# A two-layer diffusion backbone: conditioning loads issued further ahead, with their products kept in written order, and a pause in attention

## The chip, the cores and the metric

The kernel runs on one core of one Trainium2 chip. The metric is the device time of one execution in microseconds, lower is better. TensorE (PE) does the matrix products, VectorE (DVE), ScalarE (ACT) and GpSimd (POOL) the rest. SyncE (SP) issues the loads of the network's weights, and ACT issues the loads of the conditioning weights from its own queue. Each engine works off its instructions in a fixed order, so an instruction that waits holds up everything behind it on its engine.

## The reference, cut to what matters

There are 256 latent tokens, 256 context tokens, a width of 2048 and two layers. Layer 0 mixes tokens by neighbourhood attention with 16 heads, layer 1 by a gated MLP (gMLP). A SwiGLU FFN of width 5632 follows each of them. Every sub-layer takes a shift, a scale and a gate from a conditioning vector:

```python
sh1, sc1, g1, sh2, sc2, g2 = split(silu(c) @ ada_w[i] + ada_b[i], 6)   # per layer i
a = h * (1 + sc1) + sh1
y = mixer(a)                      # attention in layer 0, gMLP in layer 1
h = layer_norm(ALPHA * h + g1 * y)
h = layer_norm(ALPHA * h + g2 * swiglu(h * (1 + sc2) + sh2))
```

The product with `ada_w` has one row on the left. It is some 12 million multiplications per layer and reads 100 MB of weights per layer, and this kernel gives most of it to DVE, not to PE.

## The kernel before, in words

**Precision and the weight pipeline.** Every large product is made of three TensorE products (`mm3`, lines 87 to 90): a float32 operand is split into a rounded part and a rest, and high by high, low by high and high by low are added. A weight tile of 128x1024 floats (512 KB) is loaded by SP (line 110) into one of four `raw` buffers, rounded by ACT (`split_into`, line 93, tiles `hw...`), and subtracted by DVE (line 94, tiles `lw...`). PE consumes the pair. There are three to five such pairs, so DVE and ACT can be up to about four tiles ahead of PE. In the names, `wq`, `wk`, `wv` are the projections, `wo` the attention's output, `wt` and `wf` the FFN's first matrix, `wd` its second, `wg` and `wgo` those of the gMLP.

**Stages.** First comes a prologue that makes layer 0's first shift and scale on PE and DVE and projects the first keys and values. Then come the attention heads with their projections, the output projection `wo` with residual and layer norm, FFN 0, the gMLP with its output `wgo`, FFN 1, and the store. An output projection (`project_out`) works on two halves of the output columns; between the first half and the second it needs the gate (`need(key)`, line 741), and it has its layer norm done per 128 tokens (`finish`).

**Conditioning tasks.** All other shifts, scales and gates are made of small tasks that stand in a list beside the main work. For a shift or scale, `dot_task` (line 142) multiplies a transposed 128x1024 tile of `ada_w` with the broadcast conditioning vector and adds up each row: one DVE instruction at line 152, tiles `ad`, with a short read of the accumulator behind it. A vector takes 32 of them, and 128x16 additions at the end. For a gate, `gate_task` (line 162) adds tile times column to an accumulator of 128x2048: one DVE instruction at line 176, tiles `ag`. After 32 of those, `sum_task` (line 188) adds the 128 partitions by one GpSimd instruction, `partition_all_reduce` (line 191). In a name such as `ad1061`, the digits are layer, vector (0 to 5 for SH1, SC1, G1, SH2, SC2, G2), tile and half.

`tick` (line 216) is called at each step of the main work. It adds to a credit that `pace` set so that the listed tasks are spread over so many steps, and runs a task for each half unit of credit. `fetch_ahead` (line 197) issues the loads of the first `FETCH` tasks in the list, so a load is written that many tasks ahead of its use. The buffers are `ADA` in number (line 76). A load waits on ACT's queue until its buffer is free. `need` runs all tasks up to the ones that it names at once.

**The order of the instructions.** The program is written in order, but a scheduler may move instructions of one engine past each other by priority and by when it believes their operands to be there. An instruction that goes through `keep_in_program_order` (`pin`, line 84) is left at its place. The loads of the conditioning tiles are pinned (line 77). The DVE instructions that use them aren't.

**Attention.** For each head, the key projection (from head 3 on) and the query projection are made in steps of one weight tile each. After each step `unit` (line 475) calls `tick`, and takes one stage of the attention from the list `pend`. A head has three stages: `scores` (scores on PE, bias and maximum on DVE, exponential on ACT, reciprocal on DVE, scaling on ACT, which leaves the probabilities `p`), `transpose` (eight 128x128 transposes on PE, tiles `pt`, line 552, then a split) and `values` (12 products of 256 columns, tiles `o`). At heads 3, 7 and 11 eight steps of value projection (`proj_v`) follow. After the last head the remaining stages are run without steps between them.

Of the kernel before, what the change touches and what calls it, by code (L numbers as in the profile page):

```python
# [15 lines left out]
ALU = mybir.AluOpType  # L16
# [21 lines left out]
SH1, SC1, G1, SH2, SC2, G2 = range(6)  # L38
HK0 = 3
RAW = 4  # L40
ADA = 4
FETCH = 3
BUSY = 0.3
DVE0 = 3
W0 = HK0 * P + 512
# [6 lines left out]
def hybrid_kernel(ctx: ExitStack, tc: tile.TileContext, i, out):  # L52
    nc = tc.nc
    V, S, T = nc.vector, nc.scalar, nc.tensor
# [29 lines left out]
    def pin(ins):  # L84
        return tc.keep_in_program_order(ins)
# [54 lines left out]
    loaded = {}  # L140

    def dot_task(layer, t, nt, half):
        key = (layer, t, nt, half)

        def fetch():
            src = i["ada_t"][dot_index(layer, t, nt)]
            loaded[key] = load(src[:, half * 1024 : (half + 1) * 1024], f"ad{layer}{t}{nt}{half}")

        def run():
            r = loaded.pop(key)  # L150
            o = (cols2 if half else cols)[:, layer, t, :]
            V.scalar_tensor_tensor(  # L152
                r, r, 1.0, c_bc[:, half * 1024 : (half + 1) * 1024], ALU.mult, ALU.mult,
                accum_out=o[:, nt : nt + 1],
            )
            if nt == KT - 1 and half:
                o = cols[:, layer, t, :]
                V.tensor_tensor(o, o, cols2[:, layer, t, :], ALU.add)
                V.tensor_tensor(o, o, badj[:, layer, t, :], ALU.add)
        return [(layer, t), 0.5, run, fetch]  # L160

    def gate_task(layer, t, kt, half):
        key = (layer, t, kt, half)
        sl = slice(half * 1024, (half + 1) * 1024)

        def fetch():
            if kt == 0 and half == 0:
                g = outer.tile([P, D], F32, tag="gate", name=f"gate{layer}{t}")
                gate[(layer, t)] = g
                nc.gpsimd.memset(g, 0.0)  # L170
                nc.gpsimd.dma_start(g[0:1, :], i["ada_b_row"][layer, t : t + 1, :])
            loaded[key] = load(i["ada_g"][gate_index(layer, t, kt)][:, sl], f"ag{layer}{t}{kt}{half}")

        def run():
            g = gate[(layer, t)][:, sl]
            V.scalar_tensor_tensor(g, loaded.pop(key), c_col[:, kt, 0:1], g, ALU.mult, ALU.add)  # L176
        return [(layer, t), 0.5, run, fetch]

    def act_split(src, name, at=None):
# [23 lines left out]
    def add_tasks(layer, *ts):  # L203
        for t in ts:
            if t in (G1, G2):
                tasks.extend(gate_task(layer, t, k, e) for k in range(KT) for e in range(2))
                tasks.append(sum_task(layer, t))
            else:
                tasks.extend(dot_task(layer, t, k, e) for k in range(KT) for e in range(2))
# [67 lines left out]
    with tc.tile_pool(name="attnX", bufs=1) as px, ExitStack() as late:  # L277
# [187 lines left out]
        def t_tile(name):  # L465
            return mp.tile([P, 512], F32, tag="t", name=name, bufs=2)

        add_tasks(0, G1, SH2, SC2)
        add_tasks(1, SH1)
        pace(126)  # L470
        pend = []
        with tc.tile_pool(name="attnB", bufs=1) as pb:
            qh, ql = {}, {}

            def unit(n=1.0):
                tick(n)
                if pend:
                    pend.pop(0)()

            def proj_q(h):  # L480
                ps = acc_tile(f"qps{h}")
# [42 lines left out]
            def attention(h):  # L524
# [42 lines left out]
                        mm3(ps[:, 0:NT], vh[:, kb, :], vl[:, kb, :], th[:, ks], tl[:, ks], kb == 0, kb == 3)  # L567
                    S.copy(oT[:, h, :], ps[:, 0:NT])

                return [scores, transpose, values]  # L570

            for h in range(NH):
                if h >= HK0:
                    proj_k(h)
                proj_q(h)
                if h in V_AT_Q:
                    while len(pend) > 3:
                        pend.pop(0)()
                    proj_v(V_AT_Q[h])
            while pend:  # L580
                pend.pop(0)()

    need((0, SH2), (0, SC2))
    main = ctx.enter_context(tc.tile_pool(name="main", bufs=1))
# [249 lines left out]
    )  # L834
    affine_tasks(h_t, i["ln_row"][0], "a0")
    add_tasks(0, G2)
    add_tasks(1, SC1, SH2, SC2)
    pace(245)
    m2 = []

# [199 lines left out]
```

## Time and profile before

| | us |
|---|---|
| median of 3 runs (2460.63 to 2463.62) | 2462.59 |
| profiled execution, its own time | 2464.19 |
| profiled execution, span of the core | 2462.4 |
| PE busy | 2388.5 (97%) |
| DVE busy | 1753.7 (71%) |
| ACT busy | 1120.5 (46%) |
| read from HBM | 606.46 MB |

In the trace each instruction has its engine, its line and its operands. In square brackets stands the idle time of the engine just before the instruction, and what ended it. Busy shares alone don't tell here what a step is worth: PE is busy nearly throughout, and what can be won is its idle time. For each idle stretch of PE one has to follow what came last, often through two engines.

### The profile page before, as it was taken

To read this page: it belongs to the slowest core of one execution; us is meant where nothing else is said; L and a number is where in the kernel's file an instruction comes from. 1 tells how busy PE (TensorE), PEld (TensorE's weight loads), DVE (VectorE), ACT (ScalarE), POOL (GpSimd) and SP (SyncE) were. 2 spreads that over 40 slices of the span, in tenths; PEclk is the share of its full clock that TensorE was granted. 3 is DMA by queue.
4 is the path that set the end of the run, shared out by engine and by line. 5 is a ranking of instruction groups with operands and counts; after the bars stand their busy time and mean duration, and the time that the engine had idled before them with its cause. 6 is when DMAs were issued, how large, how long until landed. Compare 5 with 4: busy or idle time off the path is not lost. (4 is left out here: it accounts for less than half of the span.)

```text
span 2462.4 us, 31266 instructions
## 1 busy us (share of the span) xinstructions
PE 2388.5 (97%) x11574; PEld 1979.4 (80%) x11574; DVE 1753.7 (71%) x2158; ACT 1120.5 (46%) x1534; POOL 110.3 (4%) x54
## 2 busy tenths in 40 slices
PE   7999999999999999999999999899999999999998
PEld 5788888888788888887888778777888888888886
DVE  4878877777887777666778778778755555566666
ACT  3344434335554444443455554445544444445453
POOL 0000200000010010000000010020100000020000
PEclk9999999999999999999999999999999999999999
DMA  9978787877578888887888767766567676766563
GB/s 358 346 248 266 254 288 260 273 253 246 188 241 284 293 280 299 284 290 275 280 290 283 247 208 263 241 210 196 199 229 229 226 227 225 230 198 190 178 211 131
DMA packets 167682, 610.63 MB, mean 248 GB/s; under 512 B 19076, under 2 KB 21572, under 8 KB 163172
## 3 DMA queue, kind: packets, MB, share of 16 engines
q1 hardware_dynamic: 120888, 440.64, 53.9%
q10 hardware_dynamic: 46512, 167.96, 19.9%
q8 instruction: 90, 1.47, 0.2%
q14 instruction: 64, 0.52, 0.1%
q0 software_dynamic: 128, 0.03, 0.0%
HBM read 606.46 MB, written 2.10 MB: 247 GB/s over the span
## 5 line engine op out<-in xcount | busy, mean ns | idle before, releaser
L93 ACT CAST hwf<-rwf 128x1024 fp32r<-128x1024 f32 x320 | 336.9, 1053 | 491.2 <-PE pu L90 206.0
L94 DVE TENSOR_TENSOR lwf<-rwf,hwf 128x1024 fp32r<-128x1024 f32 x320 | 404.3, 1277 | 173.8 <-ACT hwf L93 172.8
L152 DVE SCALAR_TENSOR_TENSOR ad<-ad,c_bc 128x1024 f32<-128x1024 f32 x192 | 234.0, 1222 | 168.9 <-DMA ad<-in_ada_t 168.3
L88 PE MATMUL pod<-hwd,ghd 128*128 128x512 f32 x684 | 267.3, 391 | 3.5 <-DVE sg L815 3.5
L90 PE MATMUL pod<-hwd,gld 128*128 128x512 f32 x684 | 266.5, 390 | 0.7 <-DVE gld L94 0.7
L89 PE MATMUL pod<-lwd,ghd 128*128 128x512 f32 x684 | 266.8, 390 | 0.0
L176 DVE SCALAR_TENSOR_TENSOR gate<-ag,c_col,gate 128x1024 f32<-128x1024 f32 x128 | 164.4, 1288 | 121.1 <-DMA ag<-in_ada_g 120.8
L94 DVE TENSOR_TENSOR lwd<-rwd,hwd 128x1024 fp32r<-128x1024 f32 x172 | 211.7, 1232 | 51.3 <-ACT hwd L93 51.0
L93 ACT CAST hwd<-rwd 128x1024 fp32r<-128x1024 f32 x172 | 180.3, 1049 | 33.3 <-PE pu L90 11.5
L88 PEld LDWEIGHTS pod<-hwd,ghd 128*128 128x128 f32 x684 | 128.7, 188 | 30.5 <-DVE sg L815 4.0
L90 PEld LDWEIGHTS pod<-hwd,gld 128*128 128x128 f32 x684 | 128.7, 188 | 28.1 <-DVE gld L94 1.2
L89 PEld LDWEIGHTS pod<-lwd,ghd 128*128 128x128 f32 x684 | 128.8, 188 | 26.6
L88 PE MATMUL pg<-hwf,f1h 128*128 128x512 f32 x320 | 126.4, 395 | 0.0
L88 PE MATMUL pg<-hwf,f0h 128*128 128x512 f32 x320 | 126.4, 395 | 0.0
L90 PE MATMUL pg<-hwf,f1l 128*128 128x512 f32 x320 | 124.7, 390 | 0.0
L90 PE MATMUL pg<-hwf,f0l 128*128 128x512 f32 x320 | 124.7, 390 | 0.0
L88 PE MATMUL pu<-hwf,f0h 128*128 128x512 f32 x320 | 124.5, 389 | 0.0
L89 PE MATMUL pu<-lwf,f0h 128*128 128x512 f32 x320 | 124.5, 389 | 0.0
L90 PE MATMUL pu<-hwf,f0l 128*128 128x512 f32 x320 | 124.5, 389 | 0.0
L88 PE MATMUL pu<-hwf,f1h 128*128 128x512 f32 x320 | 124.5, 389 | 0.0
L89 PE MATMUL pu<-lwf,f1h 128*128 128x512 f32 x320 | 124.5, 389 | 0.0
L90 PE MATMUL pu<-hwf,f1l 128*128 128x512 f32 x320 | 124.5, 389 | 0.0
(338 smaller groups left out, 5345.1 us busy)
## 6 DMA issues: line engine op xcount, KB each, us to landing
rwf<-in_w_in_t SPq DMA_DIRECT2D x320, 512.0 KB
ad<-in_ada_t ACTq DMA_DIRECT2D x192, 512.0 KB
rwd<-in_w_out SPq DMA_DIRECT2D x176, 512.0 KB
ag<-in_ada_g ACTq DMA_DIRECT2D x128, 512.0 KB
rwg<-in_w_gin SPq DMA_DIRECT2D x64, 512.0 KB
ap<-in_ada_p SPq DMA_DIRECT2D x19, 1024.0 KB
rwq<-in_w_q SPq DMA_DIRECT2D x32, 512.0 KB
rwo<-in_w_o SPq DMA_DIRECT2D x32, 512.0 KB
```

Of the source, the lines that this page charges most:

```text
L88: keep(T.matmul(ps, sh, mh, start=first, stop=False))
L89: keep(T.matmul(ps, sh, ml, start=False, stop=False))
L90: keep(T.matmul(ps, sl, mh, start=False, stop=last))
L93: S.copy(hi, src)
L94: V.tensor_tensor(lo, src, hi.bitcast(F32), ALU.subtract)
L152: V.scalar_tensor_tensor(r, r, 1.0, c_bc[:, half * 1024 : (half + 1) * 1024], ALU.mult, ALU.mult, accum_out=o[:, nt : nt + 1],)
L176: V.scalar_tensor_tensor(g, loaded.pop(key), c_col[:, kt, 0:1], g, ALU.mult, ALU.add)
```

## The change

Six things are edited.

1. `FETCH` goes from 3 to 5 and `ADA` from 4 to 6: a load is written five tasks ahead of its use, into one of six buffers. To make room in the memory on the chip, the descriptor area of GpSimd's DMAs is cut to 4096 bytes.
2. The DVE instruction of every dot and gate task is pinned.
3. The 32 dots of layer 1's SH1 leave the attention's list and stand in the list of FFN 0. The attention has 97 tasks where it had 129, FFN 0 has 161 where it had 129, over the same `pace`.
4. In the attention's list, gate G1 stands last; it stood first.
5. An empty stage stands between `scores` and `transpose`, so that a step's work is done between the two that wasn't.
6. Before a value projection, `pend` is cut to 8 stages, not to 3.

```diff
-ADA = 4
-FETCH = 3
+ADA = 6
+FETCH = 5
+SCRATCH = 4096
...
# dot_task.run()
-            V.scalar_tensor_tensor(
+            pin(V.scalar_tensor_tensor(
                 r, r, 1.0, c_bc[:, half * 1024 : (half + 1) * 1024], ALU.mult, ALU.mult,
                 accum_out=o[:, nt : nt + 1],
-            )
+            ))
...
# gate_task.run()
-            V.scalar_tensor_tensor(g, loaded.pop(key), c_col[:, kt, 0:1], g, ALU.mult, ALU.add)
+            pin(V.scalar_tensor_tensor(g, loaded.pop(key), c_col[:, kt, 0:1], g, ALU.mult, ALU.add))
...
# ahead of the attention
-        add_tasks(0, G1, SH2, SC2)
-        add_tasks(1, SH1)
+        add_tasks(0, SH2, SC2, G1)
         pace(126)
...
+            def advance():
+                stage = pend.pop(0)
+                if stage:
+                    stage()
+
             def unit(n=1.0):
                 tick(n)
                 if pend:
-                    pend.pop(0)()
+                    advance()
...
-                return [scores, transpose, values]
+                return [scores, None, transpose, values]
...
                 if h in V_AT_Q:
-                    while len(pend) > 3:
-                        pend.pop(0)()
+                    while len(pend) > 8:
+                        advance()
                     proj_v(V_AT_Q[h])
             while pend:
-                pend.pop(0)()
+                advance()
...
# ahead of the first FFN
     add_tasks(0, G2)
-    add_tasks(1, SC1, SH2, SC2)
+    add_tasks(1, SH1, SC1, SH2, SC2)
     pace(245)
...
-    nc = bacc.Bacc("TRN2", target_bir_lowering=False, num_devices=1)
+    nc = bacc.Bacc("TRN2", target_bir_lowering=False, num_devices=1, dynamic_dma_scratch_size=SCRATCH)
```

The diff alone doesn't tell what the scheduler made of it. Three places of the DVE order show it. Line numbers of the changed kernel are one higher from line 43 to 467 and five higher from line 480 on.

**DVE at head 12's softmax, before.** `ql12` is the split of the head's query, `s120` and `s121` its scores for two blocks of queries, `nm` their maxima, `sm` their sums:

```order
L493 SCALAR_TENSOR_TENSOR ql12_4588<-qps12_4523,qh12_4587 128x256
L152 SCALAR_TENSOR_TENSOR ad1061_4592,cols2_72<-ad1061_4592,c_bc_98 128x1024
L152 SCALAR_TENSOR_TENSOR ad1070_4626,cols_71<-ad1070_4626,c_bc_98 128x1024
L535 TENSOR_TENSOR s120_4633<-s120_4633,bias12_4631 128x256
L535 TENSOR_TENSOR s121_4645<-s121_4645,bias12_4631 128x256
L537 TENSOR_REDUCE nm120_4638<-s120_4633 128x1
L537 TENSOR_REDUCE nm121_4650<-s121_4645 128x1
L94 TENSOR_TENSOR lwq13_1024_4660<-rwq13_1024_4657,hwq13_1024_4659 128x1024
L152 SCALAR_TENSOR_TENSOR ad1071_4629,cols2_72<-ad1071_4629,c_bc_98 128x1024
L541 RECIPROCAL sm120_4640<-sm120_4640 128x1
```

The loads of `ad1061`, `ad1070` and `ad1071` stand next to each other on ACT, right behind the rounding of `qh12`, that is behind the instruction on which `ql12` waits:

```order
L93 CAST hwq13_0_4597<-rwq13_0_4595 128x1024
L492 ACTIVATE qh12_4587<-qps12_4523 128x256
L77 DMA ad1061_4592<-in_ada_t 128x1024
L77 DMA ad1070_4626<-in_ada_t 128x1024
L77 DMA ad1071_4629<-in_ada_t 128x1024
```

**DVE at the same place, after:**

```order
L498 SCALAR_TENSOR_TENSOR ql12_4513<-qps12_4451,qh12_4512 128x256
L177 SCALAR_TENSOR_TENSOR gate02_3798<-ag0280_4367,c_col_58,gate02_3798 128x1024
L177 SCALAR_TENSOR_TENSOR gate02_3798<-ag0281_4406,c_col_58,gate02_3798 128x1024
L177 SCALAR_TENSOR_TENSOR gate02_3798<-ag0290_4409,c_col_58,gate02_3798 128x1024
L540 TENSOR_TENSOR s120_4558<-s120_4558,bias12_4556 128x256
L542 TENSOR_REDUCE nm120_4563<-s120_4558 128x1
L540 TENSOR_TENSOR s121_4570<-s121_4570,bias12_4556 128x256
L542 TENSOR_REDUCE nm121_4575<-s121_4570 128x1
L95 TENSOR_TENSOR lwq13_1024_4585<-rwq13_1024_4582,hwq13_1024_4584 128x1024
L546 RECIPROCAL sm120_4565<-sm120_4565 128x1
```

The tasks are now gate tasks, three in a row ahead of `s120`. Their loads stand further up on ACT; the last of the three, and what lies between it and `qh12`:

```order
L78 DMA ag0290_4409<-in_ada_g 128x1024
L94 CAST hwq12_1024_4413<-rwq12_1024_4411 128x1024
L78 DMA ag0291_4442<-in_ada_g 128x1024
L78 DMA ag02100_4445<-in_ada_g 128x1024
L94 CAST hwk13_0_4454<-rwk13_0_4452 128x1024
L94 CAST kh12_4447<-kps12_4374 128x512
L94 CAST hwk13_1024_4484<-rwk13_1024_4482 128x1024
L94 CAST hwq13_0_4522<-rwq13_0_4520 128x1024
L497 ACTIVATE qh12_4512<-qps12_4451 128x256
```

Between the load of `ag0290` and the rounding of `qh12`, four weight tiles and the keys of head 12 are rounded; before, no weight tile stood between the load of `ad1061` and its use. Over the whole program, counted in weight tiles of 128x1024 that are rounded between a load and its use, the attention's tasks had a mean of 0.3 before and have 3.9 now, those of FFN 0 had 1.0 and have 7.4, those of the gMLP 1.6 and 10.9.

**DVE at the end of attention, before.** `s150` and `s151` are the scores of the last head, `lwo` a weight tile of the output projection:

```order
L152 SCALAR_TENSOR_TENSOR ad10150_5167,cols_71<-ad10150_5167,c_bc_98 128x1024
L94 TENSOR_TENSOR lwo0_2_0_5324<-rwo0_2_0_5321,hwo0_2_0_5323 128x1024
L493 SCALAR_TENSOR_TENSOR ql15_5218<-qps15_5135,qh15_5217 128x256
L535 TENSOR_TENSOR s150_5226<-s150_5226,bias15_5224 128x256
L535 TENSOR_TENSOR s151_5238<-s151_5238,bias15_5224 128x256
L537 TENSOR_REDUCE nm150_5231<-s150_5226 128x1
L537 TENSOR_REDUCE nm151_5243<-s151_5238 128x1
L648 TENSOR_TENSOR caf0_5295<-lncol_70,cols_71 128x16
L649 TENSOR_TENSOR cbf0_5296<-lncol_70,cols_71 128x16
```

**DVE at the end of attention, after.** `vl15` is the split of the last head's values, a subtraction of two SBUF operands:

```order
L177 SCALAR_TENSOR_TENSOR gate02_3798<-ag02151_4962,c_col_58,gate02_3798 128x1024
L95 TENSOR_TENSOR lwo0_2_0_5229<-rwo0_2_0_5226,hwo0_2_0_5228 128x1024
L498 SCALAR_TENSOR_TENSOR ql15_5107<-qps15_5026,qh15_5106 128x256
L177 SCALAR_TENSOR_TENSOR gate02_3798<-ag02150_4858,c_col_58,gate02_3798 128x1024
L540 TENSOR_TENSOR s150_5131<-s150_5131,bias15_5129 128x256
L540 TENSOR_TENSOR s151_5143<-s151_5143,bias15_5129 128x256
L542 TENSOR_REDUCE nm150_5136<-s150_5131 128x1
L542 TENSOR_REDUCE nm151_5148<-s151_5143 128x1
L95 TENSOR_TENSOR vl15_5174<-v3_4369,vh15_5173 128x512
L546 RECIPROCAL sm150_5138<-sm150_5138 128x1
```

The last gate product of G1 (`ag02150`) now stands right ahead of the last head's softmax, and the reduce of GpSimd waits for this product only. The split `vl15` came well before `s150`; now it stands between the maxima and the reciprocal `sm150`.

**DVE at the end of FFN 0, before.** `yd` and `h_t` are the residual, `std0` the statistics of the layer norm, `mvm10` and `rsm10` its mean and inverse deviation for the first 128 tokens:

```order
L603 TENSOR_TENSOR yd003_11939<-pod0110_10966,gate05_6270 128x512
L604 SCALAR_TENSOR_TENSOR h_t_5292<-h_t_5292,yd003_11939 128x512
L605 BN_STATS std0_9892<-h_t_5292 128x6
L609 BN_AGGR mvm10_11954<-std0_9892 128x2
L612 RECIPROCAL rsm10_11956<-rsm10_11956 128x1
L603 TENSOR_TENSOR yd012_11998<-pod0101_10965,gate05_6270 128x512
L615 SCALAR_TENSOR_TENSOR rsm10_11956<-mvm10_11954,rsm10_11956 128x1
L604 SCALAR_TENSOR_TENSOR h_t_5292<-h_t_5292,yd012_11998 128x512
L623 TENSOR_SCALAR h_t_5292<-h_t_5292,rsm10_11956 128x512
```

**DVE at the end of FFN 0, after:**

```order
L608 TENSOR_TENSOR yd003_11939<-pod0110_10955,gate05_6172 128x512
L609 SCALAR_TENSOR_TENSOR h_t_5197<-h_t_5197,yd003_11939 128x512
L610 BN_STATS std0_9866<-h_t_5197 128x6
L153 SCALAR_TENSOR_TENSOR ad14150_11692,cols_71<-ad14150_11692,c_bc_98 128x1024
L153 SCALAR_TENSOR_TENSOR ad14151_11740,cols2_72<-ad14151_11740,c_bc_98 128x1024
L614 BN_AGGR mvm10_11954<-std0_9866 128x2
L608 TENSOR_TENSOR yd012_11998<-pod0101_10954,gate05_6172 128x512
L159 TENSOR_TENSOR cols_71<-cols_71,cols2_72 128x16
L95 TENSOR_TENSOR lwg41_1024_12084<-rwg41_1024_12081,hwg41_1024_12083 128x1024
L160 TENSOR_TENSOR cols_71<-cols_71,badj_60 128x16
L617 RECIPROCAL rsm10_11956<-rsm10_11956 128x1
```

Two dots of layer 1's SC2, with their two 128x16 additions, are run by `need` between the statistics and their aggregation, and a weight split has moved ahead of the reciprocal.

## The prediction

> **What bounds the kernel now.** I read the page's head first, then PE's waits, then the waits of the engine that PE waits for, then one wait after another in the timeline. The page's head:
>
> ```profile
> span 2462.4 us, 31266 instructions
> PE 2388.5 (97%) x11574; PEld 1979.4 (80%) x11574; DVE 1753.7 (71%) x2158; ACT 1120.5 (46%) x1534; POOL 110.3 (4%) x54
> ```
>
> PE is the bound, and the change takes no product from it. What can be won is PE's idle time, 74 us, part of which is start and end. PE's waits (engine, line, waited for: us in total, times, longest), the ones that matter here, and the two waits of DVE that feed them:
>
> ```profile
> PE pt L552 <- ACT p L542: 13.4, 7, 5.0
> PE sp L881 <- DVE u L882: 5.0, 2, 3.0
> PE pod L88 <- DVE sg L815: 3.5, 1, 3.5
> PE gu L89 <- DVE lwg L94: 3.3, 1, 3.3
> PE gv L90 <- DVE m1l L94: 3.0, 2, 2.6
> PE ztm L665 <- DVE h_t L623: 2.2, 1, 2.2
> PE vps L89 <- DVE lwv L94: 2.1, 2, 1.7
> ...
> DVE ad L152 <- DMA ad<-in_ada_t: 168.3, 103, 5.5
> DVE gate L176 <- DMA ag<-in_ada_g: 120.8, 72, 4.6
> ```
>
> PE waits for DVE and ACT, and DVE stands 289 us waiting for conditioning loads. One case shows the link (start, duration, engine, instruction, idle before). The softmax of head 12:
>
> ```profile
> 512.77 1.23 DVE L152 SCALAR_TENSOR_TENSOR ad<-ad,c_bc 128x1024 f32<-128x1024 f32 x1 [4.18 <-DMA ad<-in_ada_t]
> 515.02 1.23 DVE L152 SCALAR_TENSOR_TENSOR ad<-ad,c_bc 128x1024 f32<-128x1024 f32 x1 [1.01 <-DMA ad<-in_ada_t]
> 516.17 0.76 DVE L535 TENSOR_TENSOR s<-s,bias 128x256 f32<-128x256 f32 x2
> 520.31 0.22 DVE L541 RECIPROCAL sm<-sm 128x1 f32<-128x1 f32 x2
> ...
> 520.51 1.33 ACT L542 ACTIVATE p<-p,sm 128x512 f32<-128x512 f32 x2 [1.50 <-DVE sm L541]
> ...
> 517.91 0.39 PE L90 MATMUL kps<-ah,lwk 128*128 128x512 f32 x1
> 518.13 0.28 PE L88 MATMUL qps<-ah,hwq 128*128 128x256 f32 x1
> 518.25 0.28 PE L89 MATMUL qps<-al,hwq 128*128 128x256 f32 x1
> 521.28 0.55 PE L552 MATMUL pt<-ident,p 128*128 128x128 f32 x2 [2.64 <-ACT p L542]
> ```
>
> The two dots ahead of the softmax waited 5.19 us for their loads, the softmax behind them came late, and PE stood 2.64 us in front of the transposes. Products start every 0.22 us (512 columns) or 0.12 us (256).
>
> An idle PE also costs clock afterwards. Stretches of the trace (us, busy time of PE, PEld, DVE, ACT, POOL, PE's granted clock, DMA share, GB/s), first three stages, then 5 us around two waits of PE, of 2.64 and 2.35 us:
>
> ```profile
> 160.00:600.00 440.00, 421.47 (x2336) 366.19 (x2336) 341.08 (x509) 186.08 (x303) 12.77 (x1) 0.99 0.80 266
> 745.00:1400.00 655.00, 650.72 (x2902) 538.11 (x2901) 476.52 (x580) 294.84 (x360) 12.78 (x1) 1.00 0.84 284
> 1400.00:1600.00 200.00, 186.37 (x808) 150.88 (x807) 156.34 (x188) 96.12 (x130) 20.08 (x18) 0.97 0.70 236
> 520.00:525.00 5.00, 3.72 (x19) 3.72 (x20) 5.00 (x11) 3.82 (x6) 0.00 (x0) 0.66 0.33 108
> 566.00:571.00 5.00, 4.35 (x37) 4.33 (x38) 5.00 (x8) 4.39 (x7) 0.00 (x0) 1.00 0.60 187
> ```
>
> After 2.64 us the clock is at 0.66 over 5 us, which is 1.7 us lost. After 2.35 us it stays full. So I add 1.7 us to each wait of 2.4 us or more. Over 1400 to 1600 the loss is 200 x 0.03 = 6 us, four such falls. [...]
>
> **The change part by part.**
>
> *Lookahead and pins together.* In the old order a dot stood right behind its own load, in spite of a lookahead of three, since the scheduler moved the unpinned dot up. In the new order about four weight tiles lie between load and use in attention and seven or more later. A tile is 12 products of 0.22 us on PE, so that is some 10 us and more, against waits of at most 5.5 us. I take nearly all 289 us of DVE's waits as gone. DVE isn't the bound, so only what PE waited behind them counts.
>
> *Attention's transposes.* The 13.4 us of `pt` hold one wait of 5.0 us with another cause (below). The other 8.4 us go: the loads have landed, and the empty stage lets PE make 24 products of 512 and 24 of 256 columns between scores and transposes, 8.2 us, where it had 24 and 3, 5.6 us. This softmax took 5.0 us from 516.17 until its first half was scaled (520.51 + 0.67); with one more product ahead of it, 1.2 us, it still fits. With two falls of the clock (3.4 us): 11.8 us gained. `vps` (2.1 us) lies among the same waits; I take half, 1.0.
>
> *FFN 0.* `pod` waited 3.5 us for `sg`, behind dots that waited; with clock 5.2 us gained. The 32 dots of SH1 come in: 32 x 1.23 = 39 us of DVE, which was busy 476.5 of 655 us, then 79%; PE has four tiles of stock, so nothing on the path. Their 16.8 MB raise 284 GB/s to 310, the DMA share from 0.84 to 0.92. I take 1 us for both, with 0 and 6 as ends (one wait like that of `sg`).
>
> *gMLP.* The waits of `gv` (2.65), of `sp` (3.0 and 1.9) and of `gu` (3.3) lie behind these:
>
> ```profile
> 1436.93 1.28 DVE L176 SCALAR_TENSOR_TENSOR gate<-ag,c_col,gate 128x1024 f32<-128x1024 f32 x1 [4.46 <-DMA ag<-in_ada_g]
> 1562.12 1.29 DVE L176 SCALAR_TENSOR_TENSOR gate<-ag,c_col,gate 128x1024 f32<-128x1024 f32 x1 [2.83 <-DMA ag<-in_ada_g]
> 1616.54 1.28 DVE L176 SCALAR_TENSOR_TENSOR gate<-ag,c_col,gate 128x1024 f32<-128x1024 f32 x1 [1.89 <-DMA ag<-in_ada_g]
> ```
>
> The first three go: 2.65 + 3.0 + 1.9 with two falls of clock, 11.0 us. At `gu` DVE was simply full, after some 3 us of such waits; I take 60% of 5.0, 3.0 us. The end of the gate's list comes three steps later, and the reduce with it; PE's stock is the same there, so 0.
>
> *The reduce of G1 moves.* Its place now, another reduce, and the mean of a split of values in attention (x16, busy us, mean ns):
>
> ```profile
> 260.31 12.77 POOL L191 PARTITION_ALL_REDUCE gate<-gate  x1 [108.43 <-DVE gate L176]
> ...
> 261.59 0.43 DVE L535 TENSOR_TENSOR s<-s,bias 128x256 f32<-128x256 f32 x1 [0.26 <-PE s L90]
> 264.41 6.46 DVE L94 TENSOR_TENSOR lwk<-rwk,hwk 128x512 fp32r<-128x512 f32 x1
> ...
> 272.89 0.69 PE L552 MATMUL pt<-ident,p 128*128 128x128 f32 x2 [5.03 <-ACT p L542]
> ...
> 1638.61 12.78 POOL L191 PARTITION_ALL_REDUCE gate<-gate  x1 [93.11 <-DVE gate L176]
> ...
> 1639.61 9.30 DVE L94 TENSOR_TENSOR glgo<-uT,ghgo 128x256 fp32r<-128x256 f32 x1
> ...
> L94 DVE TENSOR_TENSOR vl<-v,vh 128x512 fp32r<-128x512 f32 x16 | 11.0, 685 | 0.4 <-ACT vh L93 0.4
> ```
>
> A split of two SBUF operands that is issued while the reduce runs is held until 10.3 to 10.6 us after the reduce's start (1648.9 and 270.9). An addition that reads PSUM (261.59) isn't held. So the 5.0 us at 272.89, with its clock 6.7, go from this place. In the new order the reduce starts when `ag02150` ends, the last head's additions and maxima read PSUM and pass, and `vl15` (two SBUF operands) is held until 10.4 us after the start, with the reciprocals behind it. With 0.7 for the split and 0.9 for reciprocal and scaling, `p` is there 12.0 us after it. PE, when `ql15` is done, still has two products of scores and 19 of the output projection ahead of the transposes (21 x 0.22 = 4.6 us), and up to 2.7 us more of `o14`, scores and projection. `ag02150` (1.3) comes first on DVE, so PE arrives 3.3 to 6.0 us after the reduce's start and waits 6.0 to 8.7 us; I take the middle, 7.4, and 1.7 of clock: 9.1. Net cost 2.4 us. Were the split to slip in before the reduce takes hold, the new wait would be 0. [...]
>
> *The end of FFN 0.* `need` now puts two dots and a weight split into the chain that ends in PE's wait `ztm`:
>
> ```profile
> 1408.07 0.26 DVE L609 BATCH_NORM_AGGREGATE mvm<-std 128x2 f32<-128x24 f32 x1
> 1408.70 0.16 DVE L612 RECIPROCAL rsm<-rsm 128x1 f32<-128x1 f32 x1 [0.36 <-ACT rsm L611]
> 1410.09 0.54 DVE L623 TENSOR_SCALAR h_t<-h_t,rsm 128x512 f32<-128x512 f32 x1
> 1411.15 1.21 DVE L94 TENSOR_TENSOR lwg<-rwg,hwg 128x1024 fp32r<-128x1024 f32 x1
> ```
>
> PE has nothing else there: it already waits 2.2 us. Two dots are 2.5 us and the split 1.2. The 0.36 us in which DVE waited take some of it, two small additions and a residual product that now stand ahead of the reciprocal add about as much: 3.7 us longer. Bounds 2.5 (the dots alone) and 4.3 (a residual product of 0.6 added).
>
> *The rest.* The smaller descriptor area touches four loads of 8 KB on GpSimd, the larger stock only memory, the limit of 8 stages only when heads 2 and 3 run: 0.
>
> Sum: 11.8 + 1.0 + 5.2 + 11.0 + 3.0 = 32.0 gained; 2.4 + 1.0 + 3.7 = 7.1 lost; 24.9 us. From the profiled execution's own 2464.2 (its span is 2462.4, the rest lies around it) that gives 2439.3. It lay 1.6 us above the median, so 2437.7, rounded 2438. The gains left out (waits under 0.4 us behind the same loads) make me lean lower rather than higher.
>
> **The rivals.** *Loads late for another reason.* If loads are late because the engines that move them are full, depth helps little: the queue only grows. FFN 0 decides it, where 310 GB/s are asked for. At 284 GB/s, what it had, 16.8 MB take 59 us more; 24.9 - 5.2 = 19.7 gained elsewhere would leave 2502, and it is slower than before as soon as a third of that shows: 186 + 16.8 MB in 655 + 20 us, a rate below 300 GB/s. Against it: in its first two slices the core moved 358 and 346 GB/s,
>
> ```profile
> GB/s 358 346 248 266 254 288 260 273 253 246 188 241 284 293 280 299 284 290 275 280 290 283 247 208 263 241 210 196 199 229 229 226 227 225 230 198 190 178 211 131
> ```
>
> and the dots that waited had been issued only a few us before. Chance 0.05, slower. [...]
>
> *Only attention gains.* If the waits in FFN 0 and the gMLP come from DVE's own load, which grows, and not from the loads of tiles: 12.8 - 7.1 = 5.7 us, 2457. For it: at `gu` DVE was full. Against: the three rows above. Chance 0.12, at the edge of what counts as faster.
>
> *The reduce costs nothing at its new place.* The split would then pass as the addition at 261.59 does, PE would not wait there, and the time would be 9.1 less, 2429. For it: only that the split could be issued early. Chance 0.1.
>
> *Nothing happens*, because the pins change no waits: 2462. The new order speaks against it. Chance 0.04, same.
>
> **How the numbers follow.** The forecast's own case has 0.69. Its bounds: FFN 0 +5, the reduce +1, `gu` and `vps` -3 and +4, the chain -1 and +1, small waits -5; not all at once, that makes 2430 to 2447. With the free reduce below and part of the second rival above, the range is 2424 to 2453. About 0.2%, 5 us, is what a measurement of this kernel can tell from no change. Faster has 0.69 + 0.1 and two thirds of 0.12, 0.87; same 0.04 and the other third, 0.08; slower 0.05.
>
> **What would show it.** DVE's waits for `ad` and `ag` together under 60 us; `pt` with one long wait only, near 580 us, of 7 to 8 us, behind a `vl` of 8 us beside the reduce; no wait for `sg`; `ztm` at the end of FFN 0 near 6 us. I am wrong if the waits for `ad` stay above 150 us, if `hwf` or `lwf` become what PE waits for in FFN 0, or if PE's idle time falls and the time doesn't.

## The result, and the profile after

The changed kernel takes 2443.91 us (median of four runs, 2442.75 to 2446.65) against 2462.5 us for the kernel before; the ratio is 0.9928, 95% interval 0.9912 to 0.9944. That is 18.6 us faster; the forecast was 24.5 us, 2438. The profiled execution took 2446.65 us, so against the 2464.2 us of before it gained 17.5 us, where the sum said 24.9.

The head of the page of the changed kernel:

```profile
span 2444.9 us, 31279 instructions
PE 2381.0 (97%) x11574; PEld 1977.7 (81%) x11574; DVE 1764.2 (72%) x2158; ACT 1122.7 (46%) x1534; POOL 109.7 (4%) x54
```

PE still does the same 11574 products; it only stands less. Where the time came from is read best by stage. This table takes the start of the first product of each stage from the timeline of PE (first `qps`, `pg` of FFN 0, `gv`, `pg` of FFN 1, last product) and gives the lengths between them, in us; the forecast is the sum of the prediction's terms for the stage.

| stage | before | changed | difference | forecast |
|---|---|---|---|---|
| attention and output projection | 507.8 | 490.3 | -17.5 | -10.4 |
| FFN 0 | 745.4 | 742.5 | -2.9 | -0.5 |
| gMLP | 300.2 | 294.7 | -5.5 | -14.0 |
| FFN 1 | 736.1 | 744.6 | +8.5 | 0 |

So the total was nearly met by two stages that gained more than forecast and two that gained less or lost. Each length is of one execution; in a second execution of the changed kernel (below) the gMLP took 289.9 us, the other stages 490.3, 743.0 and 746.1. The waits of the changed kernel (engine, line, waited for: us in total, times, longest):

```profile
PE pod L89 <- DVE sg L820: 7.7, 1, 7.7
PE pt L557 <- ACT p L547: 6.7, 1, 6.7
PE sp L886 <- DVE u L887: 4.2, 1, 4.2
PE pogo L91 <- DVE glgo L95: 3.0, 2, 2.0
PE ztm L670 <- DVE h_t L628: 3.0, 1, 3.0
...
PE gv L89 <- ACT m1h L94: 2.1, 1, 2.1
...
DVE ad L153 <- DMA ad<-in_ada_t: 0.9, 2, 0.5
```

DVE's waits for conditioning loads fell from 289 us to 0.9, and `ag` is not in the list at all. The transposes have one wait instead of seven. But the list has a new head: 7.7 us for `sg` in FFN 1, where PE had no wait before the change.

The forecast wait first. The end of attention in the timeline (start, duration, engine, instruction, idle before), head 15's softmax:

```profile
549.38 1.27 DVE L177 SCALAR_TENSOR_TENSOR gate<-ag,c_col,gate 128x1024 f32<-128x1024 f32 x1
550.57 0.76 DVE L540 TENSOR_TENSOR s<-s,bias 128x256 f32<-128x256 f32 x2
550.76 11.88 POOL L192 PARTITION_ALL_REDUCE gate<-gate  x1 [398.97 <-DVE gate L177]
552.43 7.99 DVE L95 TENSOR_TENSOR vl<-v,vh 128x512 fp32r<-128x512 f32 x1
560.35 0.15 DVE L546 RECIPROCAL sm<-sm 128x1 f32<-128x1 f32 x1
...
561.30 0.69 PE L557 MATMUL pt<-ident,p 128*128 128x128 f32 x2 [6.67 <-ACT p L547]
```

It is the chain of the prediction, row by row: the last gate product, the reduce, additions that read PSUM and pass (0.76 us for the two, as at 516.17 before, with no reduce beside them), the split `vl` that is held (7.99 us where it takes 0.7), the reciprocals behind it, PE idle for 6.67 us.

Now the wait that was not forecast, at the end of FFN 1's up products:

```profile
2178.90 1.28 DVE L177 SCALAR_TENSOR_TENSOR gate<-ag,c_col,gate 128x1024 f32<-128x1024 f32 x1
2180.28 11.88 POOL L192 PARTITION_ALL_REDUCE gate<-gate  x1 [440.13 <-DVE gate L177]
2180.47 10.00 DVE L95 TENSOR_TENSOR lwd<-rwd,hwd 128x1024 fp32r<-128x1024 f32 x1 [0.30 <-ACT hwd L94]
2190.40 1.27 DVE L820 TENSOR_TENSOR sg<-pu,sg 128x512 f32<-128x512 f32 x2
...
2191.13 0.80 PE L89 MATMUL pod<-hwd,ghd 128*128 128x512 f32 x1 [7.70 <-DVE sg L820]
```

and the same reduce in the kernel before:

```profile
2167.72 12.77 POOL L191 PARTITION_ALL_REDUCE gate<-gate  x1 [400.73 <-DVE gate L176]
2169.44 12.78 DVE L94 TENSOR_TENSOR lwf<-rwf,hwf 128x1024 fp32r<-128x1024 f32 x4 [0.69 <-ACT hwf L93]
...
2209.59 1.28 DVE L815 TENSOR_TENSOR sg<-pu,sg 128x512 f32<-128x512 f32 x2
```

Before, the reduce began 42 us ahead of the last `sg` and held a weight split for which PE did not have to wait (four splits share the 12.78 us). Now it begins 10 us ahead of it. In DVE's order 16 weight splits stood between the last product and this `sg`; now there is one, it is held for 10.00 us, and `sg`, which the first product of `w_out` needs, waits behind it.

### The profile page after: what moved, and what is told of

Same layout as the page of the kernel before. It is cut to its first block, busy times and chain, and to the rows that moved or that the text cites. A ratio compares the mean times of both kernels' runs of the same rounds, so it can differ in the third digit from the quotient of the medians.

```text
span 2444.9 us, 31279 instructions
## 1 busy us (share of the span) xinstructions
PE 2381.0 (97%) x11574; PEld 1977.7 (81%) x11574; DVE 1764.2 (72%) x2158; ACT 1122.7 (46%) x1534; POOL 109.7 (4%) x54
## 5 line engine op out<-in xcount | busy, mean ns | idle before, releaser
L95 DVE TENSOR_TENSOR lwd<-rwd,hwd 128x1024 fp32r<-128x1024 f32 x172 | 220.4, 1283 | 67.8 <-ACT hwd L94 67.8
```

The lines of the kernel that those rows point to most:

```text
L95: V.tensor_tensor(lo, src, hi.bitcast(F32), ALU.subtract)
```

## Experiments

All ratios are to the kernel before on the same chip, with 95% intervals. The kernel before had medians of 2465.6 to 2470.1 us beside the experiments and 2462.5 beside the first result; the changed kernel stayed at 2443.4 and 2443.9. Why the kernel before varies more is open. So kernels from different chips are compared by their ratios and, more finely, by the length of a stage in their traces. Each such length is of one execution: in the gMLP kernels with nothing changed there lie up to 7 us apart (288.7 to 295.9), in the other three stages most are within 1 to 2 us.

**The changed kernel again** (no edit).

> The changed kernel as it is, beside the next two on one chip. Both theories: ratio to before 0.990 to 0.994, the same waits as in its first run (p 6.7, sg 7.7).

2443.35 us, ratio 0.9905 (0.9886 to 0.9924). Waits of 6.6 us for `p` and 7.7 for `sg`. The gMLP took 289.9 us in this execution, 4.8 less than in the first.

**Without the pins.**

```
-            pin(V.scalar_tensor_tensor(
+            V.scalar_tensor_tensor(        # dots and gate products alike
```

> The changed kernel without the pins on dots and gate products; depth, lists and empty stage stay. In its order a dot stands 0.3 weight tiles behind its load in attention and 1.2 in FFN 0 again (3.9 and 7.6 with pins), and the last gate product of FFN 1 some 29 rows earlier on DVE. Theory (the pins give the lead; they also move the last reduce to the end of FFN 1's gate and up products, where PE waits 7.7 us and loses 3.4 of clock): DVE's waits for ad and ag go back to 200 to 300 us, the wait for sg at 2191 goes; 2443.9 - 11 + 15 to 28 = 2448 to 2461, I expect 2453. Rival (depth alone gives the lead): waits stay under 20 us and the time is 2433 to 2444.

2453.58 us, ratio 0.9950 (0.9932 to 0.9968). The waits:

```profile
DVE ad L153 <- DMA ad<-in_ada_t: 149.3, 97, 5.1
DVE gate L177 <- DMA ag<-in_ada_g: 104.2, 60, 4.8
```

253 us of waits are back in spite of the deeper lookahead, and the wait for `sg` in FFN 1 is gone: the stretch from the first product of `w_out` to the end is 240.2 us, 251.0 with pins. Both halves of the theory hold: the pins give the lead, and they move the last reduce. It starts 425.4 us after the stage's first product, with pins 492.1; the other three start 7, 16 and 17 us earlier in their stages than with pins.

**The pins alone.**

```
 # the kernel before
-            V.scalar_tensor_tensor(
+            pin(V.scalar_tensor_tensor(    # dots and gate products alike
```

> The kernel before with the pins alone. A dot stands 1.7 tiles behind its load in attention, 5.9 in FFN 0. Theory: ad and ag together fall from 289 to under 80 us; the reduce of G1 stays near 260 us with its wait of 5 us; a wait of PE for sg of 7 to 8 us comes at the end of FFN 1's up products, since the pins alone move the last reduce there. 2462.5 - 17 (attention's small waits and clock, half of them) - 5 (FFN 0) - 5 (gMLP) + 11 = 2447, range 2443 to 2456. Rival (the new wait for sg comes from the depth, not the pins): no wait for sg, 2436 to 2445.

2448.15 us, ratio 0.9912 (0.9897 to 0.9928), by which it can't be told from the whole change (0.9928 and 0.9905). The waits:

```profile
PE pod L88 <- DVE sg L815: 7.7, 1, 7.7
...
DVE gate L176 <- DMA ag<-in_ada_g: 3.2, 1, 3.2
...
DVE ad L152 <- DMA ad<-in_ada_t: 2.6, 2, 2.3
```

With the old depth the conditioning waits are 6 us, and the wait for `sg` is there in full. It is the pins' doing. The waits of the transposes for `p` are down to 0.6 us in all, so the pins removed those too. By stages: attention 497.2 us (before 507.8, changed 490.3), FFN 0 741.3, gMLP 290.0, FFN 1 744.2. In its trace the pins alone lack 6.9 us of the attention's gain.

**The old depth.**

```
-ADA = 6
-FETCH = 5
+ADA = 4
+FETCH = 3
```

> The changed kernel with the old depth (ADA 4, FETCH 3); pins, lists and empty stage stay. A dot stands 2.4 weight tiles behind its load in attention and 4.7 in FFN 0. Theory (the pins do it, a tile is 2.9 to 5.4 us, so two tiles are more than the longest wait of 5.5): ad and ag together under 30 us, time 2442 to 2447, 2444. Rival (the depth is needed as well): waits of over 60 us in attention, time 2448 to 2456.

2444.52 us, ratio 0.9899 (0.9883 to 0.9915); attention 490.4 us.

```profile
DVE ad L153 <- DMA ad<-in_ada_t: 2.1, 2, 1.2
DVE gate L177 <- DMA ag<-in_ada_g: 0.4, 1, 0.4
```

By the ratio the deeper lookahead, first in the change's name, is worth nothing here that can be measured once the instructions are pinned. In the trace it may be worth some 3 us in FFN 0, which took 746.0 us here and 742.5 and 743.0 in the two executions of the changed kernel: there is a wait that they don't have:

```profile
PE pod L89 <- DVE sg L820: 2.2, 1, 2.2
```

One execution with the deeper lookahead (both reduces moved, below) has a wait of 1.3 us at the same place, so this isn't settled.

**The old lists.**

```
-        add_tasks(0, SH2, SC2, G1)
+        add_tasks(0, G1, SH2, SC2)
+        add_tasks(1, SH1)
...
-    add_tasks(1, SH1, SC1, SH2, SC2)
+    add_tasks(1, SC1, SH2, SC2)
```

> The changed kernel with the old lists: G1 first in attention, then SH2, SC2, SH1; FFN 0 without SH1. Pins, depth and empty stage stay. Theory: the reduce is back near 260 us, with a wait of 5 us and 1.7 of clock in place of 6.7 and 2.2 near 561, so 2 us gained there; 39 us of dots come back to attention, whose waits are gone, and cost 0 to 3 us; the wait for sg in FFN 1 stays. 2441 to 2446, 2442. Rival (the move of the 32 dots is what frees attention): attention has waits for p of over 5 us besides the reduce's, 2449 to 2456.

2446.83 us, ratio 0.9911 (0.9896 to 0.9926), just above the theory's band. The reduce is at 264.2 us again and costs PE

```profile
PE kps L91 <- DVE lwk L95: 5.7, 1, 5.7
```

and attention takes 490.9 us, 0.6 more than with the new lists. So the move of the reduce and of the 32 dots is worth about nothing either way: 2 us of gain were expected and not seen. But no wait for `p` came back, which speaks against the rival.

**Without the empty stage.**

```
-                return [scores, None, transpose, values]
+                return [scores, transpose, values]
```

> The changed kernel without the empty stage between scores and transposes; the rest stays. Theory (with the pins the dots no longer wait, and the softmax of 5.0 us fits behind the 5.6 us of products that the old stages had): no wait for p but that of the reduce at the end of attention, attention from first q to FFN 0 within 3 us of 490.3; ratio to before 0.992 to 0.994. Rival (the empty stage is what removed the 8.4 us of waits for p): waits for p of 4 us or more besides the reduce's, ratio 0.995 to 0.998, 5 to 12 us above the changed kernel.

2449.59 us (2444.40 to 2451.77), ratio 0.9915 (0.9897 to 0.9932), just below the theory's band and overlapping the repeat of the changed kernel. In absolute time it is 6 us above the changed kernel, as the rival had it, but the kernel before took longer on this chip too (2470.05). The trace is of the fastest of the six executions. There attention takes 491.9 us, 1.6 more, and there is no wait for `p`. At its end the reduce now holds a tiny addition of two SBUF tiles, and PE waits for the weight split behind it:

```profile
554.51 7.48 DVE L653 TENSOR_TENSOR caf<-lncol,cols 128x16 f32<-128x16 f32 x1
```

```profile
PE powo L90 <- DVE lwo L95: 6.5, 1, 6.5
```

The empty stage did not remove the waits for `p`. With the pins the softmax fits behind the products that stood there before.

Between the pins alone (497.2 us in attention) and the old lists with depth and empty stage (490.9) lie 6.3 us, while depth and empty stage are each worth 0 to 1.6 when taken out of the whole change. In the lists of PE's waits 3.8 of the 6.3 us are seen, 1.5 of them for `lwv` at the first value projection and 1.3 for `tl` ahead of `o`. Whether depth or empty stage is enough for them stays open. The two kernels also differ in the limit on `pend` before a value projection (8 or 3 stages), which no run changes alone.

**FFN 1's reduce earlier.**

```
-    pace(170)
+    pace(156)
```

> The changed kernel with pace(156) in place of pace(170) for FFN 1's gate: its last product stands 14 rows earlier on DVE, about 11 weight tiles ahead of the end of the up products. Theory (the reduce holds a split of w, sg waits behind it on DVE, PE waits 7.7 us for sg and then runs at half clock): that wait goes, and the stretch from the first product of w_out to the end falls from 251 to 240 us; 10.8 us less than the changed kernel, ratio to before 0.988 to 0.990. Rival (sg is late at this place because DVE is full): a wait of over 4 us for sg or gld stays, ratio 0.991 to 0.993.

2433.33 us, ratio 0.9855 (0.9836 to 0.9873), below the theory's band. From the first product of `w_out` to the end 240.1 us, 10.8 less, and no wait for `sg`:

```profile
2136.12 11.88 POOL L192 PARTITION_ALL_REDUCE gate<-gate  x1 [402.03 <-DVE gate L177]
```

```profile
2136.32 13.41 DVE L95 TENSOR_TENSOR lwf<-rwf,hwf 128x1024 fp32r<-128x1024 f32 x4 [0.30 <-ACT hwf L94]
```

The reduce holds a split as long as ever (the four take 13.41 us; three at 1.14, as from 586.95 to 588.09 in the next kernel's trace, leave 10.0 for the first), but PE has tiles in stock there: from 2100 us on, its list of waits is empty. Only the gate's list of FFN 1 was moved, so the wait and its clock, 10.8 us, are this reduce's place.

**Attention's reduce later.**

```
-        pace(126)
+        pace(134)
```

> The changed kernel with pace(134) in place of pace(126) in attention: the last products of G1 and its reduce fall some 25 rows later, into the output projection, where four weight tiles are in stock and no softmax is left. Theory: the wait for p of 6.7 us near 561 goes with 2.2 of clock; the reduce holds a split of wo or of oT instead, which costs 0 to 3; the stretch from first q to FFN 0 falls from 490.3 to 481 to 485, ratio to before 0.9885 to 0.9910. Rival (the hold costs as much wherever it falls): a wait of 5 us or more in the output projection, ratio 0.992 to 0.994.

2438.83 us, ratio 0.9878 (0.9859 to 0.9897), just below the theory's band. The traced execution is the slowest of the five (2444.77 us). In it attention and output projection take 486.5 us, 3.8 less; in the next two kernels, which have the same edit, 483.8 and 484.9. The wait for `p` is gone, but the theory's 5 to 9 us were mostly too much, since the output projection splits its left operand just ahead of use:

```profile
578.00 9.03 DVE L95 TENSOR_TENSOR glwo<-oT,ghwo 128x256 fp32r<-128x256 f32 x1 [0.23 <-ACT ghwo L94]
```

```profile
PE powo L91 <- DVE glwo L95: 3.0, 2, 2.2
```

**Both reduces moved** (the two edits above).

> The changed kernel with both reduces moved: pace(134) in attention and pace(156) in FFN 1. Theory: the two gains add, 7 + 10.8 = 18 us less than the changed kernel, near 2426 where before is 2462; ratio to before 0.984 to 0.987. Rival (one of the two places only moves its wait): ratio 0.988 to 0.991.

2431.81 us, ratio 0.9849 (0.9830 to 0.9869). The stages show both gains: attention 483.8 us, FFN 1 733.9. The total doesn't: by the ratio this kernel can't be told from the one with FFN 1's reduce moved alone (0.9855), and in the traced executions the gMLP took 293.5 us here and 288.7 there.

**FFN 0's last dots out of the chain as well.**

```
 # both reduces moved, and
-    pace(245)
+    pace(242)
```

> Both reduces moved (pace 134 in attention, 156 in FFN 1) and FFN 0's list a little faster, pace(242) in place of 245: the last two dots stand 15 rows ahead of the residuals of FFN 0's last block, not in the chain of its layer norm. Theory (the two dots lengthen the chain by 2.5 us and bring a longer fall of the clock): the wait of PE for h_t falls from 3.0 to under 2 us and the 10-us fall of the clock there shortens; 2 to 4 us less than with the two reduces moved alone, ratio to before 0.982 to 0.985. Rival (the chain is bound by PE's last products and the activations, not by the dots): the wait stays at 2 to 3 us, gain under 1 us.

2427.03 us, ratio 0.9836 (0.9818 to 0.9854), the best here and clear of the changed kernel's 0.9905. FFN 0 takes 738.4 us, 5.3 less than with both reduces moved and 4.0 to 6.7 less than in the seven executions with the same lists and pace(245) (742.4 to 745.1). The waits of PE around FFN 0's end:

```profile
PE gv L89 <- ACT m1h L94: 1.6, 2, 1.4
PE ztm L670 <- ACT zsm L676: 0.5, 1, 0.5
PE ztm L670 <- DVE h_t L628: 0.4, 1, 0.4
```

The wait for `h_t` fell from 3.0 to 0.4 us. The two dots that `need` put into the layer norm's chain are the cause of it. Of the 5.3 us, 1.3 are another matter: a wait for `sg` near 1142 us that the execution with both reduces moved had and this one hasn't. By its last product this execution is only 2.3 us ahead of the one with both reduces moved, because its gMLP took 1.6 us more and its start and attention together 1.3; the two ratios overlap.

**Pins and one pace.**

```
 # the kernel before with the pins, and
-    pace(170)
+    pace(156)
```

> The kernel before with the pins and pace(156) in FFN 1, nothing else of the change: old lists and depth, no empty stage. Theory (the pins hold the gain, the place of the last reduce the loss): waits for ad and ag under 10 us, no wait for sg over 2 us, the stretch from the first product of w_out in FFN 1 to the end near 240 us; 10 us less than the changed kernel, ratio to before 0.986 to 0.989. Rival (depth, lists or the empty stage carry part of the gain): ratio 0.990 or above.

2438.14 us, ratio 0.9886 (0.9869 to 0.9904). The end of FFN 1 without idle time of PE (us, busy time of PE, PEld, DVE, ACT, POOL, clock, DMA share, GB/s):

```profile
2184.79:2424.92 240.13, 240.13 (x1064) 198.75 (x1063) 159.76 (x200) 117.10 (x173) 5.39 (x2) 1.00 0.57 181
```

Two edits, pins and one number, do as well as the whole change did as it was made (0.9905 on the same chip). That doesn't make the rest worthless: with the same pace the whole change had 0.9855, and its attention took 490.3 us where it takes 497.2 here. So the rival is right in part: by the traces depth, lists, empty stage and the limit on `pend` together carry some 7 us in attention.

**The gMLP without its gate products.** The wait for `u` stayed in every kernel so far. This one skips 28 of the 32 products of the gMLP's gate (28 x 1.28 = 36 us of DVE; the 29 in the expectation is a slip) and keeps their loads.

```
+            if (layer, t) == (1, G1) and kt < 14:
+                loaded.pop(key)
+                return
```

> The changed kernel, in which 28 of the 32 gate products of G1 in the gMLP (29 us busy by prediction rows of 1.28 us, 36 us) are left out of the computation; their loads, of the same bytes in the same order, and the reduce stay. Theory (in the gMLP DVE is full, and it is the products themselves that make u late at 1536, not late loads): the wait of PE for u of 3 to 4 us falls under 1 us with its clock, and the stretch from the first product of the gMLP to FFN 1 falls from 294.7 to 286 to 290; ratio to before 0.985 to 0.989. Rival (casts wait for loads of w_gin because the conditioning loads fill the same engines): the wait for u stays at 2 us or more, ratio 0.989 to 0.992.

2436.8 us, ratio 0.9892 (0.9862 to 0.9922). PE doesn't wait for `u` at all, and the gMLP takes 284.8 us, against 294.7 and 289.9 in the two executions of the changed kernel and 288.7 at the least in the other kernels. The 56 us ahead of that wait, changed kernel first, then this one:

```profile
1480.00:1536.00 56.00, 52.62 (x233) 43.28 (x231) 48.14 (x59) 26.74 (x30) 5.41 (x6) 0.99 0.73 254
```

```profile
1480.00:1536.00 56.00, 56.00 (x251) 45.77 (x250) 42.96 (x60) 28.77 (x36) 5.07 (x6) 1.00 0.81 273
```

ACT's casts wait for their weight loads as before, 33.3 us in all in the changed kernel, 40.0 here:

```profile
ACT hwg L94 <- DMA rwg<-in_w_gin: 40.0, 24, 6.1
```

So with less work on DVE the late weight loads don't make `u` late. The ratio is at the edge between the two theories; the wait decides. It doesn't show that the loads have no part in it. In the changed kernel the last instructions ahead of `u` are

```profile
1533.94 1.23 DVE L95 TENSOR_TENSOR lwg<-rwg,hwg 128x1024 fp32r<-128x1024 f32 x1 [1.56 <-ACT hwg L94]
1535.09 1.28 DVE L177 SCALAR_TENSOR_TENSOR gate<-ag,c_col,gate 128x1024 f32<-128x1024 f32 x1
1536.28 0.87 DVE L887 SCALAR_TENSOR_TENSOR u<-sp,bs,u 128x256 f32<-128x256 f32 x2
```

a split that waited 1.56 us for a cast, and a gate product. Whether earlier weight loads would end the wait as well, no run shows.

## Why the prediction was right, and where its steps were not

**DVE's waits go (right).** Under 60 us were forecast, 0.9 measured. The cause was named half rightly: it was not lookahead and pins together, the pins alone do it (6 us of waits with the old depth, 253 without pins).

**Attention (right, under-sized).** The gain was 17.5 us for 10.4. The terms for `pt` were met, but the other short waits went too. Before, the named waits of this stage summed to 18.5 us, and three falls of the clock at 1.7 made 5.1 more; now the waits are 7.4 us and the clock 2.2. That is 14.0 us, 3.6 more than forecast, most of it `vps`, `qps`, `kps` and `o`, of which I took half of one; the other 3.5 us lie in gaps too short for the list of waits. The empty stage, on which I hung the 8.4 us, isn't what removed them: the pins alone left 0.6 us of waits for `p`.

**The reduce at its new place (right).** 7.4 us of wait and 1.7 of clock were forecast, 6.7 and 2.2 measured. Two errors partly cancel in the 7.4. I had `p` ready 12.0 us after the reduce's start, and it was 10.5: the 10.3 to 10.6 us were already the ends of held splits, so the 0.7 for the split was counted twice, and this reduce lasted 11.88 us where those lasted 12.8. And PE arrived 3.9 us after the start, near the early end of the 3.3 to 6.0. The rival in which the reduce costs nothing is out. A net cost of 2.4 us against the old place was forecast; with the old lists attention took 0.6 us more, not less.

**FFN 0 (right in sign).** No wait for `sg` in FFN 0, and the 32 dots cost at most 0.6 us up to its output projection. The rival of loads that come late for the DMA engines falls: over FFN 0 the core moved 302 GB/s instead of 278 (us, busy time by engine, clock, DMA share, GB/s; before, then changed),

```profile
668.58:1413.93 745.35, 735.78 (x3289) 607.04 (x3289) 551.44 (x673) 346.95 (x442) 26.39 (x12) 1.00 0.82 278
```

```profile
651.02:1393.52 742.50, 734.50 (x3288) 606.10 (x3289) 595.02 (x739) 350.25 (x445) 27.19 (x13) 1.00 0.88 302
```

and all the waits for dots come to 0.9 us. The chain at its end was to grow by 3.7 us, and it grew by 3.5. From the end of the last statistics to the first `h_t` it is 5.6 us now,

```profile
1383.45 0.69 DVE L610 BATCH_NORM_STATS2 std<-h_t 128x6 f32<-128x512 f32 x1
1389.70 0.54 DVE L628 TENSOR_SCALAR h_t<-h_t,rsm 128x512 f32<-128x512 f32 x1
```

and was 2.1. What failed is that PE has nothing else there: it had products for another 3.3 us behind these statistics, where before it had 0.5. So `ztm` waits 3.0 us and not 6; the wait of `gv` behind it grew from 1.4 to 2.1, and the fall of the clock there from 3.4 us at half clock (from 1415.76 on) to 6.8 (from 1391.70 on). Moving the dots out again gives 4 to 5 us.

**gMLP (wrong).** "The first three go: 2.65 + 3.0 + 1.9 with two falls of clock, 11.0 us." The wait of `gv` for 2.65 us went, and that of `gu` went whole (3.3 us, of which I took 60%). Of those for `u`, 3.0 and 1.9 us, one of 4.2 us is left. I took the late load in front of each wait for its cause. It was what DVE did last; without it DVE had the same work (busy 46.5 of the 56 us ahead of the wait before, 48.1 now) and was late anyway, and only taking out the gate products ended the wait. That was the rival in which the waits come from DVE's own load, which I had priced for all stages or none. "The reduce with it; PE's stock is the same there, so 0" failed too: the wait for `glgo` went from 1.0 to 3.0 us (2.6 in the second execution). The size of the miss is less sure than its cause: 8.5 us by the first execution, 3.7 by the second.

**FFN 1 (missing).** The sum has no term for it, and the sign "no wait for `sg`" failed here. I followed the reduce that the change moves by name and the one of the gMLP. The pins move all four, since each starts when the last product of its list is done, and the one in FFN 1 came to stand one split ahead of the `sg` that PE needs: 7.7 us and 3.1 of clock, 10.8 by the experiment that moved it back.

That the time fell into the range although two steps failed is owed to errors of both signs: 7.1 and 2.4 us more gained in the first two stages, 8.5 and 8.5 less in the others. In that the total is luck. The rule for the clock, 1.7 us for each long wait, was too simple as well (below).

## What to carry to other kernels

When an edit changes when a consumer runs, list everything that starts when the last of these consumers is done, in every stage, and look at what stands behind each in the order of the engine that it disturbs; here one number in a list's pace was worth 10.8 us, where the whole change gained 18.6. A wait for a load just ahead of a late instruction is its cause only if the engine would otherwise have been in time: compare the engine's busy share of the stretch first. And when a change has six parts, try the smallest alone: by the ratio the pins gave what the six gave together, and the 7 us that the others added in attention show only in the traces.

## What the runs showed of the hardware

The reduce on POOL held DVE instructions with two SBUF operands down to an addition of 128x16 (7.48 us without the empty stage; 0.18 in the changed kernel, where it came behind the hold), and splits for 6.5 to 10.2 us. With a reduce of 11.88 us the hold ended 9.2 to 10.2 us after its start, with one of 12.8 us 10.3 to 11.1. But it need not begin with it. Where the reduce fell into the output projection it lasted 16.05 us, and splits passed for its first 4 us:

```profile
573.46 16.05 POOL L192 PARTITION_ALL_REDUCE gate<-gate  x1 [420.62 <-DVE gate L177]
```

```profile
576.54 1.23 DVE L95 TENSOR_TENSOR lwo<-rwo,hwo 128x1024 fp32r<-128x1024 f32 x1
```

The one at 578.00 was then held until 587.0. What starts the hold isn't shown.

The clock's fall doesn't cost 1.7 us for every wait. Slices of the timeline of 1 us (us, busy time by engine, clock, DMA share, GB/s), in which the half clock after the waits of 6.67 and 7.70 us ends (the slice ahead of each has 0.50):

```profile
565.00:566.00 1.00, 1.00 (x4) 0.76 (x4) 0.96 (x2) 1.00 (x2) 0.00 (x0) 0.66 0.95 410
```

```profile
2197.00:2198.00 1.00, 1.00 (x6) 0.78 (x5) 1.00 (x2) 0.00 (x0) 1.00 (x1) 0.88 0.00 0
```

PE restarted at 561.30 and was at half clock until about 565.7, 4.4 us, 2.2 lost; at 2191.13 until 2197.2, 6.1 us, 3.1 lost. Within each trace all changes of the granted clock lie on one grid of 3.413 us. In the changed kernel the falls from the first head on begin at 558.85, 1391.70, 1535.06, 1647.70 and 2187.01 us, which is 244, 42, 33 and 158 steps apart, and they last one to three steps, 3.4, 6.8 or 10.2 us. In the kernel before, those in attention begin at 272.30, 391.76 and 521.47 us, 35 and 38 steps apart, and last one step each.

PE need not be idle for a whole step. Three steps of the grid in the kernel before, around its waits of 2.64 and 2.35 us:

```profile
518.06:521.47 3.41, 0.78 (x7) 0.53 (x6) 3.41 (x7) 1.91 (x6) 0.00 (x0) 1.00 0.51 164
562.43:565.84 3.41, 1.87 (x10) 1.43 (x8) 3.41 (x8) 1.45 (x4) 0.00 (x0) 1.00 0.37 111
565.84:569.26 3.42, 2.61 (x22) 2.59 (x23) 3.42 (x7) 3.39 (x6) 0.00 (x0) 1.00 0.48 146
```

The wait of 2.64 us lies in one step and leaves PE 0.78 us of busy time; the clock falls to 0.50 at 521.47. That of 2.35 us is shared by two steps with 1.87 and 2.61 us of busy time, and the clock stays at 1.00. It is the same over all 14 traces of this case, from 70 to 2405 us, counting the steps at full clock. A fall followed each of the 53 steps in which PE was busy for less than 1.45 us, and none of the 9362 with more than 1.82; of the 37 between, 14. In the kernel before and the changed one alone these are 12 steps, 1330, and two of five. So what a wait cost in clock here depended on where in the grid it lay, and 2.4 us, the prediction's limit, is no limit by itself.
